# The mLSTM's state update on two halves of the TensorE array: one matmul per head and one copy out of PSUM per direction

## The chip, the cores and the metric

The kernel runs on one core of one Trainium2 chip. The metric is the device time of one execution in microseconds. Before the change three runs took 3370.57, 3371.3 and 3374.14 us, a median of 3371.3 us.

## The reference: what is computed

One encoder layer of width 1024 over 2304 tokens (2048 of one request, 256 of another) with two token mixers side by side, an mLSTM with 8 heads and an attention with 8 query heads and 2 key/value heads, then an output projection, a gated convolutional feed-forward of width 2816 and a last normalisation. The change touches the mLSTM alone. Its core, for one direction (the mLSTM runs forwards and backwards over the sequence), per chunk of tokens and per head:

```python
num = iw[..., None] * jnp.einsum('bhld,bhde->bhle', qb, C) + jnp.einsum('bhls,bhse->bhle', s, vb)
den = iw * jnp.einsum('bhld,bhd->bhl', qb, n) + jnp.sum(s, axis=-1)
h = num / jnp.maximum(jnp.abs(den), jnp.exp(-m_t))[..., None]
C_new = dec[..., None, None] * C + jnp.einsum('bhs,bhsd,bhse->bhde', we, kb, vb)
n_new = dec[..., None] * n + jnp.einsum('bhs,bhsd->bhd', we, kb)
```

The state C is 64 by 64 for each head, and n is a vector of 64. The kernel holds both as one matrix of 64 by 65: a column of ones beside v makes the 65th column of the update the update of n. What the change is about is the second term of C_new and n_new, the product of weighted keys and values.

## The kernel before, in words

The kernel works on chunks of 128 tokens, 18 of them (16 of the first request, 2 of the second), and on pairs of heads, 4 of them. A pair's keys fill 128 partitions or columns: head 0 has 0 to 63, head 1 has 64 to 127. Tensors are kept in float32; where a matmul of full precision is wanted in the fast type, operands are split into a high and a low part (lines 763, 773, 789 and others); the small mLSTM matmuls of lines 842, 887, 893 and 905 take plain float32, which the hardware carries out in two passes each. So each of them stands in the trace as two weight loads and two matmuls.

The stages follow each other: the attention's and gates' projections (to about 250 us), then mLSTM and attention together (to about 1440 us), then the rest of the attention with the output projection (L1045), and from about 1800 us the feed-forward (L1202, L1531). In the second stage two generators are stepped in turn by `run_both`, which compares shares of estimated cost. Of a pair p the mLSTM generator makes: the projections of keys, queries, values and output gate (L763, L773; L789 for the last pair), `projT`, which transposes the keys (L823) and weights them on GpSimd (tile kw, L829), `upd`, which makes each chunk's update (tile mu) and copies it to C (L844, L845), `recur`, which runs the recurrence over the chunks on VectorE (L853), and then the outputs, chunk by chunk: `out_a` (exponentials, L879), `out_b` (tiles mS, L887, and mI, L893), `out_c` (tile mN, L905, and the division), `out_d` (transpose mT, L930, and the store to mix_d). While pair p's outputs are made, pair p+1 is projected. The tiles mu, mS, mI, mN, mT and mt share two PSUM buffers (`MB` = 2, tag "m").

The attention's pieces are in tiles px (a maximum, L573 and L574), ps (scores, L599 and L600), ph and pl (exponentials in two parts, L603 to L605) and pv (values, L617). L617 alternates between a stationary operand of 128 columns and one of 64.

The order of each engine's instructions is made by a scheduler that simulates the program: the mLSTM's small steps are issued under high priority (`MPRI`), and everything else fills in. A change of one instruction's size can therefore move others. In the stage with the output projection the order on TensorE is fixed by hand.

`upd` is called for every chunk and both directions d: forwards the update goes to the next chunk's state, backwards to the previous one's, and where there is none the edge state is cleared. That makes 32 updates per pair and 128 in all. Before the change one matmul multiplies both heads' keys (128 columns) with both heads' values (130 columns), giving a matrix of 128 by 130, of which only the two diagonal blocks of 64 by 65 are wanted. Two copies on ScalarE take them out.

Of the kernel before, what the change touches and what calls it, by code (L numbers as in the profile page):

```python
# [11 lines left out]
AF = mybir.ActivationFunctionType  # L12
# [706 lines left out]
def mlstm(g, tc, s1, sp, sw, sn, pj_, pm):  # L719


    nc = g.nc
# [8 lines left out]
    def weights(p):  # L731
        s = Pair()
        s.p = p
        s.hs = slice(2 * p, 2 * p + 2)
        s.w = [sw.tile([P, 2, 512], F32R, tag="w", name=f"wm{p}_{c}", bufs=WB) for c in range(NCC)] if p else g.wm0
        for c in range(NCC if p else 0):
            load_split(g, s.w[c][:, 0, :], s.w[c][:, 1, :], g.w_m[p, c], g.raw if c % RWM < 2 else sp,
                       f"rm{p}_{c}", RST, g.n1w[:, c:c + 1], bufs=2 if c % RWM < 2 else RWM - 2)
        s.kT, s.qb, s.va, s.C, s.kw = [], [], [], [], {}
        for i in range(NT):  # L740
            s.C.append(sp.tile([P, 2, 65], F32, tag="C", name=f"C{p}_{i}", bufs=NT))
        for b in range(NB):
            s.kT.append(s1.tile([P, BT], F32, tag="kT", name=f"mkT{p}_{b}", bufs=NB))
            s.qb.append(s1.tile([P, 2, 2, P], F32, tag="qb", name=f"qb{p}_{b}", bufs=NB))
            s.va.append(s1.tile([P, 2, 2, 65], F32, tag="va", name=f"va{p}_{b}", bufs=NB))
        return s
# [86 lines left out]
    def upd(s, i):  # L833
        nm = f"{s.p}_{i}"
        kw = s.kw.pop(i)
        pu = pm.tile([P, 2, 130], F32, tag="m", name="mu" + nm)
        lo, hi = SEGS[0] if i < NT1 else SEGS[1]
        for d, nx in ((0, i + 1), (1, i - 1)):
            if not lo <= nx < hi:
                nc.vector.memset(s.C[lo if d == 0 else hi - 1][:, d, :], 0.0)  # L840
                continue
            nc.tensor.matmul(pu[:, d, :], kw[:, d].rearrange("p h d -> p (h d)"),
                             s.va[i // 2][:, i % 2].rearrange("p h e -> p (h e)"), start=True, stop=True)
            nc.scalar.activation(s.C[nx][0:64, d, :], pu[0:64, d, 0:65], AF.Copy)  # L844
            nc.scalar.activation(s.C[nx][64:128, d, :], pu[64:128, d, 65:130], AF.Copy)  # L845

    def recur(s):
        for (c0, c1) in SEGS:
# [89 lines left out]
    def proj_steps(s):  # L938
        for b in range(NB + 2):
            if b < NB:  # L940
                (proj if s.p < LASTP else proj_kv)(s, b)
                if s.p == LASTP:
                    vback(s, b)
            if 2 <= b:
                with tc.high_priority(offset=MPRI):
                    upd(s, 2 * b - 4)
                    upd(s, 2 * b - 3)
            yield (6 if s.p < LASTP else 3) if b < NB else 0.5
            if 1 <= b <= NB:
                with tc.high_priority(offset=MPRI):  # L950
                    projT(s, b - 1)
            yield (6 if s.p < LASTP else 3) if b < NB else 0.5
# [25 lines left out]
    s = weights(0)  # L978
    yield from proj_steps(s)
    for p in range(4):  # L980
# [3 lines left out]
        if p < 3:  # L984
# [9 lines left out]
            s = s2  # L994
# [782 lines left out]
```

## Time and profile before

| What | Value |
|---|---|
| median of three runs | 3371.3 us |
| profiled execution, its own time | 3373.21 us |
| its span, first to last instruction | 3371.5 us |
| mean granted TensorE clock | 0.987 |
| TensorE matmul busy | 3274.1 us (97%) |
| ScalarE busy | 1779.4 us (53%) |
| VectorE busy | 2421.2 us (72%) |
| copies of the updates (L844, L845) | 256, 56.1 us busy |
| update matmuls (L842) in the trace | 256, two per update |

In the rows of the profile PE is TensorE's matmul, PEld its weight load, DVE VectorE, ACT ScalarE, POOL GpSimd and SP SyncE. A tile such as `mu<-va,kw` is output, then inputs; `128*128 128x130` behind a matmul is rows by columns of the stationary operand, and then partitions by moving columns. A matmul's duration runs from its issue to its modelled end; successive ones overlap, so that the distance between their starts, not the duration, is what each costs the engine.

### The profile page before, as it was taken

The numbers are of one execution on the slowest core, as the hardware profiler recorded it, in microseconds if no ns is written. First come the engines' busy times: TensorE is split into PE (matmuls) and PEld (weight loads), VectorE is DVE, ScalarE is ACT, GpSimd is POOL, SyncE is SP. The second block draws the span as 40 slices with busy tenths as digits, with TensorE's granted clock in tenths as the row PEclk, the third lists the DMA queues.
The fourth block names the chain that finished last, engine by engine and source line by source line (L and its number), as shares of the span: only waits on it lengthen the run. The fifth ranks groups of instructions, "written<-read, shape, count | busy, mean of one in ns | idle before, by whom it ended". The sixth has DMA issues, their size and how long they took to land. (4 is left out here: it accounts for less than half of the span.)

```text
span 3371.5 us, 57154 instructions
## 1 busy us (share of the span) xinstructions
PE 3274.1 (97%) x21402; PEld 3047.9 (90%) x21402; DVE 2421.2 (72%) x3771; ACT 1779.4 (53%) x3708; POOL 1311.9 (39%) x1672
## 2 busy tenths in 40 slices
PE   7989999999999999899999999999999999999998
PEld 6878888888888888788889999999999998999998
DVE  6975687777768778876765778878877776544573
ACT  4535666667666776665553544445555555323331
POOL 6544122213232332211245457745555442851112
PEclk9999999999999999999999999999999999999999
DMA  6766343333345444433347334325322223875573
GB/s 223 240 198 175 90 130 102 103 105 116 105 117 176 130 132 138 129 99 97 108 138 260 123 102 148 129 94 180 105 94 94 100 97 103 296 275 172 169 226 100
DMA packets 300262, 481.86 MB, mean 143 GB/s; under 512 B 36528, under 2 KB 186192, under 8 KB 299984
## 3 DMA queue, kind: packets, MB, share of 16 engines
q1 hardware_dynamic: 247600, 348.33, 32.6%
q0 software_dynamic: 35824, 120.42, 10.8%
q10 hardware_dynamic: 16560, 9.44, 0.9%
q8 instruction: 169, 2.77, 0.3%
q14 instruction: 109, 0.89, 0.1%
HBM read 336.19 MB, written 141.90 MB: 142 GB/s over the span
## 5 line engine op out<-in xcount | busy, mean ns | idle before, releaser
L605 DVE TENSOR_TENSOR pl<-ps,ph 128x512 fp32r<-128x512 f32 x520 | 353.3, 684 | 184.1 <-ACT ps L604 176.5
L1202 PE MATMUL pa<-nt,wut 128*128 128x290 f32 (+1 forms) x3168 | 448.3, 297 | 9.2 <-ACT u L1220 7.6
L1202 PEld LDWEIGHTS pa<-nt,wut 128*128 128x128 f32 x3168 | 432.4, 190 | 11.5 <-ACT u L1220 9.4
L603 ACT ACTIVATE ph<-ps 128x512 fp32r<-128x512 f32 x520 | 309.7, 596 | 246.5 <-PE ps L600 240.9
L574 DVE TENSOR_REDUCE mx<-px 128x1 f32<-128x512 f32 (+1 forms) x528 | 346.3, 673 | 73.9 <-PE px L573 71.9
L1312 DVE SCALAR_TENSOR_TENSOR y<-u,cw,y 128x1152 f32<-128x1152 f32 (+1 forms) x176 | 321.4, 1826 | 36.3 <-ACT yc L1310 17.3
L617 PE MATMUL pv<-ph,v 128*128 128x512 f32 (+1 forms) x1040 | 318.6, 400 | 1.5 <-ACT ph L603 1.3
L604 ACT ACTIVATE ps<-ps 128x512 f32<-128x512 f32 x520 | 310.1, 596 | 0.0
L1531 PE MATMUL et<-tet,wet 128*128 128x384 f32 x1584 | 279.2, 337 | 1.1 <-DVE tet L1374 1.1
L1531 PEld LDWEIGHTS et<-tet,wet 128*128 128x128 f32 x1584 | 276.9, 188 | 1.4 <-DVE tet L1374 1.4
L1045 PEld LDWEIGHTS po<-cmx,wo 128*128 128x128 f32 x1728 | 221.8, 192 | 10.0 <-DVE cmx L1033 1.5
L1045 PE MATMUL po<-cmx,wo 128*128 128x256 f32 x1728 | 226.3, 285 | 1.8 <-DVE cmx L1033 1.3
L1531 PE MATMUL e<-te,we 128*128 128x384 f32 x1188 | 212.9, 340 | 9.9 <-ACT te L1373 7.1
L1531 PEld LDWEIGHTS e<-te,we 128*128 128x128 f32 x1188 | 210.4, 190 | 11.0 <-ACT te L1373 7.3
L599 PE MATMUL ps<-qq,kk 128*128 128x512 f32 x520 | 215.4, 416 | 3.7 <-DVE mx L574 2.3
L573 PE MATMUL px<-kk,qq 128*128 128x512 f32 (+1 forms) x528 | 202.1, 412 | 5.2 <-DVE mx L574 2.9
L600 PE MATMUL ps<-qm,kl 65*128 65x512 f32 x520 | 206.8, 400 | 0.0
L763 PE MATMUL mj<-mn,wm 128*128 128x256 f32 x1296 | 202.0, 287 | 2.6 <-ACT og L777 1.9
L763 PEld LDWEIGHTS mj<-mn,wm 128*128 128x128 f32 x1296 | 185.7, 191 | 20.0 <-ACT og L777 2.0
L773 PEld LDWEIGHTS mv<-wm,mn 128*128 128x128 f32 x1296 | 184.2, 191 | 18.5 <-ACT qb L769 2.5
L773 PE MATMUL mv<-wm,mn 128*128 128x256 f32 x1296 | 197.9, 286 | 1.0 <-ACT qb L769 0.9
L617 PEld LDWEIGHTS pv<-ph,v 128*128 128x128 f32 (+1 forms) x1040 | 157.0, 163 | 38.3 <-ACT ph L603 2.6
(305 smaller groups left out, 7245.2 us busy)
## 6 DMA issues: line engine op xcount, KB each, us to landing
mn<-n_d SPq DMA_DIRECT2D x216, 256.0 KB, 3.3
ru<-w_up SPq DMA_DIRECT2D x88, 512.0 KB, 3.6
a_d<-y POOLq DMA_DIRECT2D x88, 288.0 KB, 2.6
a_d<-tc POOLq DMA_DIRECT2D x66, 288.0 KB, 3.0
n_d<-n1T SPq DMA_DIRECT2D x18, 1024.0 KB, 5.6
dm<-nm_d POOLq DMA_DIRECT2D x72, 256.0 KB, 4.0
mjn<-n_d SPq DMA_DIRECT2D x72, 256.0 KB, 3.3
mvn<-n_d SPq DMA_DIRECT2D x72, 256.0 KB, 3.2
```

Source lines behind the costliest of these rows:

```text
L574: nc.vector.tensor_reduce(s.mx[:, t, z0:z0 + 1], ps[:, 0:w], AX.X, ALU.max)
L599: nc.tensor.matmul(ps, kk[:, kc:kc + P], s.qq[:, 0:N], start=True, stop=False)
L603: nc.scalar.activation(ph, ps, AF.Exp)
L604: nc.scalar.activation(ps, ps, AF.Exp)
L605: nc.vector.tensor_tensor(pl, ps, f32(ph), ALU.subtract)
L617: nc.tensor.matmul(s.pv[0:HD if k in (1, 3) else P, 0:N], v, p, start=(kp == 0 and k == 0), stop=(2 * kp + 2 == s.nk and k == 5))
L763: nc.tensor.matmul(pj[:, o], s.w[c][:, a, o * P:(o + 1) * P], nT[c][:, :, h, :], start=(c + o + k == 0), stop=(c == NCC - 1 and k == 2 and ...
L773: nc.tensor.matmul(pv[:, o], nT[c][:, o, a, :], s.w[c][:, h, 256:512], start=(c + o + k == 0), stop=(c == NCC - 1 and k == 2 and o == 1))
L1045: nc.tensor.matmul(po[:, o], wo[z // 2][c][:, a, n], mx[c][:, h, :], start=(c == 0 and k == 0), stop=(c == NCC - 1 and k == 2))
L1202: nc.tensor.matmul(p[:, z], w[:, aa, c, :], ops[k][:, c, bb, z * m:z * m + m], start=c == 0 and i == 0 and not add, stop=c == NCC // 2 - 1 ...
L1312: nc.vector.scalar_tensor_tensor(y[:, s:e], u[:, s + k:e + k], cw[:, k, jj:jj + 1], y[:, s:e], ALU.mult, ALU.add)
L1531: nc.tensor.matmul(ps[m // 2][:, m % 2], w[:, aa, m * P:(m + 1) * P], t[:, bb], start=p == 0 and n == 0, stop=p == NP - 1 and n == 2)
```

## The change

Each update's matmul of 128 by 130 is replaced by two, one per head: head h's 64 key columns as stationary operand, placed at columns 64h of the array, and head h's 65 value columns as moving operand. The result of head h lands in partitions 64h to 64h+63 and in columns 0 to 64, for both heads. So a single copy of 128 by 65 takes both out of PSUM. The PSUM tile keeps its size. Nothing else is edited.

```diff
@@ upd(s, i), inside the loop over (d, nx) @@
-            nc.tensor.matmul(pu[:, d, :], kw[:, d].rearrange("p h d -> p (h d)"),
-                             s.va[i // 2][:, i % 2].rearrange("p h e -> p (h e)"), start=True, stop=True)
-            nc.scalar.activation(s.C[nx][0:64, d, :], pu[0:64, d, 0:65], AF.Copy)
-            nc.scalar.activation(s.C[nx][64:128, d, :], pu[64:128, d, 65:130], AF.Copy)
+            for h in range(2):
+                r = slice(64 * h, 64 * h + 64)
+                nc.tensor.matmul(pu[r, d, 0:65], kw[:, d, h], s.va[i // 2][:, i % 2, h], start=True, stop=True,
+                                 tile_position=(0, 64 * h))
+            nc.scalar.activation(s.C[nx][:, d, :], pu[:, d, 0:65], AF.Copy)
```

The diff adds one line, so that lines behind it carry numbers one higher afterwards (L905 becomes L906). TensorE issues 20,780 matmuls where it issued 20,652, ScalarE 128 instructions fewer; on the other engines the number is the same.

On TensorE, at the first updates of the first pair (a minus stands for before, a plus for the change):

```order
-L842 MATMUL mu_0_3325<-va_0_2525,kw_0_3138 128x130
-L842 MATMUL mu_1_3330<-va_0_2525,kw_1_3140 128x130
+L844 MATMUL mu_0_3325<-va_0_2525,kw_0_3138 64x65 x2
+L844 MATMUL mu_1_3330<-va_0_2525,kw_1_3140 64x65 x2
 L763 MATMUL mj_4_3785<-mn_4_0_3769,wm_0_395 128x256 x6
 L763 MATMUL mj_4_3785<-mn_4_1_3770,wm_1_508 128x256 x6
-L763 MATMUL mj_4_3785<-mn_4_2_3771,wm_2_629 128x256 x5
+L763 MATMUL mj_4_3785<-mn_4_2_3771,wm_2_629 128x256 x6
```

Each row of an update becomes two matmuls in the same place. Here two updates stand in a row; counted over the program, the 128 updates stand in 96 such groups with other matmuls between them, 32 of them of two updates. Behind 89 of these groups stands a matmul with an ordinary load of 128 columns, behind the other 7 a transpose.

On ScalarE, at the copies of those updates:

```order
-L844 ACTIVATE C_1_2506<-mu_0_3325 64x65
-L845 ACTIVATE C_1_2506<-mu_0_3325 64x65
-L844 ACTIVATE C_2_2507<-mu_1_3330 64x65
-L845 ACTIVATE C_2_2507<-mu_1_3330 64x65
+L846 ACTIVATE C_1_2506<-mu_0_3325 128x65
+L846 ACTIVATE C_2_2507<-mu_1_3330 128x65
 L603 ACTIVATE ph_0_0_0_2909<-ps_0_0_0_2906 128x512
 L604 ACTIVATE ps_0_0_0_2906<-ps_0_0_0_2906 128x512
```

Four copies of 64 partitions become two of 128, ahead of the attention's exponentials.

On TensorE again, at the last chunk's outputs of the last pair. Before:

```order
L617 MATMUL pv_8_18666<-pl_8_1_1_17561,v_16_0_11404 128x512
L905 MATMUL mN_17_18460<-va_8_13697,dm_17_18331 128x65 x4
L930 MATMUL mT_15_18480<-ident,hh_15_18399 128x128
L599 MATMUL ps_8_4_0_18703<-qq_8_17195,kk_16_8_11424 128x512
L600 MATMUL ps_8_4_0_18703<-qm_8_17197,kl_16_8_11425 128x512
```

And with the change:

```order
L617 MATMUL pv_8_18666<-pl_8_0_1_17470,v_16_0_11404 128x512
L906 MATMUL mN_17_18460<-va_8_13697,dm_17_18331 128x65 x4
L599 MATMUL ps_8_3_0_18674<-qq_8_17195,kk_16_4_11413 128x512
L600 MATMUL ps_8_3_0_18674<-qm_8_17197,kl_16_4_11414 128x512
L599 MATMUL ps_8_3_1_18682<-qq_8_17195,kk_16_4_11413 128x512
L600 MATMUL ps_8_3_1_18682<-qm_8_17197,kl_16_4_11414 128x512
```

The attention's pieces stand earlier or later against the mLSTM's: the last mN now follows the values (pl) of one pair of key blocks earlier, and attention work stands between it and mT_15. Such shifts, of up to 68 matmuls, run through the whole stage; the output projection and the feed-forward keep the order that they had but for a few rows.

## The prediction

> **What bounds the kernel now.** I read the page's head first, then the stretches of the stage in which the update stands, then the groups of the lines that the diff touches, then the waits.
>
> ```profile
> span 3371.5 us, 57154 instructions
> PE 3274.1 (97%) x21402; PEld 3047.9 (90%) x21402; DVE 2421.2 (72%) x3771; ACT 1779.4 (53%) x3708; POOL 1311.9 (39%) x1672
> core 0: us, PE busy (x) PEld busy (x) DVE busy (x) ACT busy (x) POOL busy (x), PEclk, DMA share, GB/s
> 290.00:1275.00 985.00, 979.68 (x6211) 857.89 (x6210) 739.62 (x1593) 664.53 (x1790) 260.89 (x532) 1.00 0.40 119
> 1275.00:1440.00 165.00, 154.96 (x927) 131.47 (x927) 142.77 (x355) 111.09 (x298) 47.16 (x90) 0.96 0.43 127
> ```
>
> In the stretch that holds all updates (290 to 1275 us) TensorE is busy 979.68 of 985 us at full clock. ScalarE is busy 664.53 us, two thirds of it. So the stage is as long as TensorE's list of work: a nanosecond more or less on TensorE counts nearly whole, one on ScalarE only where TensorE waits for it. TensorE's idle time there is 5.3 us, all that a faster ScalarE could win at the level of gaps.
>
> ```profile
> L842 PEld LDWEIGHTS mu<-va,kw x256: 186/189/193, 295.2 to 1273.4; 128*128 128x128 f32 x128
> L842 PE MATMUL mu<-va,kw x256: 272/274/378, 295.4 to 1273.5; 128*128 128x130 f32 x128
> L844 ACT ACTIVATE C<-mu 64x65 f32<-64x65 f32 x128 | 27.7, 217 | 46.1 <-PE mu L842 43.4 <-DMA mn<-n_d 1.3
> L845 ACT ACTIVATE C<-mu 64x65 f32<-64x65 f32 x128 | 28.4, 222 | 1.5
> ```
>
> The 128 updates are 256 passes on TensorE, and 256 copies on ScalarE that take 56.1 us. The first copy of each pair waits for TensorE, not the other way round.
>
> **The copies.** A copy of 65 columns takes 217 to 222 ns. The shape that replaces it, 128 partitions by 65, is in no row; a copy's time I take from its columns, so 128 copies of some 220 ns go and 28 us of ScalarE go with them. Their cover is named above: TensorE runs 99% of the stretch regardless. What comes out is read from the waits of TensorE and its loads on ScalarE between 290 and 1440 us, of which these name the copies or the largest of the rest:
>
> ```profile
> PE pv L617 <- ACT ph L603: 1.3, 2, 1.0
> PE mN L905 <- ACT C L845: 0.3, 1, 0.3
> PEld pv L617 <- ACT ph L603: 2.6, 5, 1.2
> PEld mN L905 <- ACT C L845: 1.2, 3, 0.7
> PEld mT L930 <- ACT C L845: 0.6, 2, 0.4
> PEld mu L842 <- ACT C L845: 0.3, 1, 0.3
> ```
>
> The waits on C come from the two PSUM buffers that mu shares with mS, mI, mN and mT: 2.4 us. An update's two directions hold their buffer for four copies today, for two afterwards, which halves them: −1.2 us. The exponentials wait behind fewer copies, worth perhaps −0.3 us of the 3.9. I take −1.5 us. Bounds: 0, and −6.3 us if all six rows vanished.
>
> **The matmuls.** What a pass costs is the distance between starts. Three pieces of the timeline show it: an update, the outputs' mN with 65 moving columns, and the transposes of L428.
>
> ```profile
> 309.25 0.42 PEld L842 LDWEIGHTS mu<-va,kw 128*128 128x128 f32 x2
> 309.60 0.19 PEld L599 LDWEIGHTS ps<-qq,kk 128*128 128x128 f32 x1
> 309.71 0.19 PEld L600 LDWEIGHTS ps<-qm,kl 65*128 65x128 f32 x1
> 309.49 0.38 PE L842 MATMUL mu<-va,kw 128*128 128x130 f32 x2
> 449.73 0.53 PEld L905 LDWEIGHTS mN<-va,dm 128*128 128x128 f32 x4
> 450.17 0.19 PEld L599 LDWEIGHTS ps<-qq,kk 128*128 128x128 f32 x1
> 450.28 0.19 PEld L600 LDWEIGHTS ps<-qm,kl 65*128 65x128 f32 x1
> 246.27 0.39 PEld L428 LDWEIGHTS gpt<-ident,rows 40*128 40x128 f32 x5
> ```
>
> Update: two matmuls in 0.38 us, one lasting 0.27, so 110 ns between them, and the next load starts 110 ns on (309.60 to 309.71). One update costs 2 x 110 = 220 ns. mN: four loads in 0.53 us of 0.19 each, 113 ns apart, and L599's load and its successor again 110 ns apart (450.17 to 450.28), though only 65 columns move. So a load of 128 float32 columns sets 110 ns, whatever moves above it.
>
> ```profile
> L617 PEld LDWEIGHTS pv<-ph,v 128*64 128x64 f32 x520 | 70.5, 136 | 15.1
> L617 PEld LDWEIGHTS pv<-pl,v 128*128 128x128 f32 x520 | 98.0, 189 | 27.7
> L905 PE MATMUL mN<-va,dm x576: 217/275/447, 449.4 to 1433.9; 128*128 128x65 f32 x192
> ```
>
> A load of 64 columns is 189 − 136 = 53 ns shorter than one of 128: it sets about 55 ns. The fastest 65-column matmul (217) is 55 ns shorter than the 130-column one (272): half the columns also stream in 55 ns. So a new pass needs 55 ns for its load and 55 ns for its stream, side by side. Whether the engine issues a load and a matmul that often, L428 answers: five loads in 0.39 us of 0.14, 62 ns apart. The pass costs 55 to 62 ns, an update four of them: 220 to 248 ns against 220. That is 0 to +28 ns, 128 times: 0 to +3.6 us, of which I take +1.8 by the middle.
>
> The last pass adds a cost of its own. Today the next matmul's load (110 ns) hides under the update's last stream of 110 ns; behind a stream of 55 ns it sticks out by 55, as behind mN. It happens once per group of updates with an ordinary load behind it, by the order 89 times: 89 x 55 ns = +4.9 us. Bounds: 0, if a free half of the array lets that load begin earlier, and the 4.9. The entrance costs nothing either way: its load hides under a predecessor of 110 ns or more. Matmuls: +6.7 us, from 0 to +8.5.
>
> **Narrow stationary operands as such.** Two rows could speak of a cost of changing the array's division. L617 alternates 128 and 64 columns 520 times. And L323, 40 columns wide, whose program gives it the same tile of 128 by 64 as the new matmuls:
>
> ```profile
> 99.40 0.14 PEld L323 LDWEIGHTS pg<-ident,gp 128*40 128x40 f32 x2
> 99.55 0.30 PEld L249 LDWEIGHTS pj<-w_a,n1T 128*128 128x128 f32 x2
> 99.44 0.38 PE L323 MATMUL pg<-ident,gp 128*40 128x128 f32 x2
> 99.57 0.48 PE L249 MATMUL pj<-w_a,n1T 128*128 128x512 f32 x1
> ```
>
> L249's load starts 110 ns after L323's second matmul (99.44 plus 0.11, the 0.38 less one duration of 0.27), and the next load 110 ns later (0.30 less 0.19). Nothing waits for an empty array, so I put the change of division at nothing. Column position 64 is in no row; that is what keeps the rival below alive.
> The Trainium skill, TensorEngine Tiling (Array Packing), section Tiling Modes, speaks against the change: changing the tiling mode drains the engine. By this rule the sum would be the drain rival's; the rows of L617 and L323 do not show it.
>
> **Order.** The scheduler moves work by up to 68 matmuls. In a stretch where TensorE is full, order is free. It is not at the end of the mLSTM, where the last outputs' chain makes TensorE wait:
>
> ```profile
> 1400.00:1420.00 20.00, 14.25 (x60) 10.58 (x61) 19.05 (x52) 12.28 (x36) 5.25 (x11) 0.74 0.26 80
> 1406.86 1.94 PE L905 MATMUL mN<-va,dm 128*128 128x65 f32 x8 [3.11 <-DVE mmx L935]
> ```
>
> VectorE is busy 19.05 of 20 us there and TensorE 14.25, at a clock of 0.74; one mN stands 3.11 us behind mmx on VectorE. With the change less attention work stands between the last mNs, and some between mN and mT_15. I can't sign this: the gaps of such a stretch, 5.75 us here, are the size of it, so ±3 us, taken as 0.
>
> **Sum.** −1.5 + 1.8 + 4.9 + 0 = +5.2 us. On the profiled execution, whose own time is 3373.21 us (its span of 3371.5 and 1.7 around it), that gives 3378.4. This execution was 1.9 us above the median of 3371.3, so for a median I say 3376.5 us, +0.15%. What this kernel's measurement can tell from no change is about 0.2%, 6.7 us.
>
> **The rivals.** *The array drains at each change of division.* An update's matmul lasts 272 ns where its successor starts after 110; the difference of about 160 ns is what an emptied array would cost, at the entrance and the exit of 96 groups: 192 x 0.16 = +31 us, with the 5.2 some 3407 us. Against it stand the rows of L617 and L323. Loads that don't overlap the streams of the other half give a like sum: four passes of 110 ns instead of 55, +220 ns x 128 = +28 us. It decides from about 35 ns per change on (6.7 us over 192). Chance 0.13.
>
> *The two heads run beside each other in the two halves.* Head 1's passes overlap head 0's and an update costs two passes of 55 ns instead of four: −110 ns x 128 = −14 us on the sum, 3362 us. For it: they share no columns. Against it: loads follow each other in one row of the trace everywhere, and four loads at 55 ns are already the 220. Chance 0.10.
> The Trainium skill says so in TensorE: Matmul & The Clock Gate, section Part 3: Packing small matmuls: matmuls in different column groups run concurrently, some 4 ns apart. No run here shows it.
>
> *ScalarE's relief or the new order wins more than TensorE loses.* The waits on ScalarE vanish whole (−6.3 instead of −1.5 us), and the chain at the end loses the 3.11 us wait and its like. −6.3 + 6.7 − 6 gives −6 us, 3365.5 us. For it speaks that ScalarE loses 28 us of 664; against it that only 2.4 us of the waits name the copies. Chance 0.15.
>
> **How the numbers follow.** The forecast has 0.62, spread over 0 to +10 us by its own bounds; about a third of that lies above the 6.7 us. Slower: 0.13 + 0.22 = 0.35. Faster: 0.07 of the concurrent case and 0.06 of the last one = 0.13. Same: the remaining 0.52. The range must hold 0.8: from 3363 us, which leaves out half of the concurrent case, to 3392, which takes in a drain of half the price and leaves the full one out. The forecast's own range is 3369 to 3382.
>
> **What would show it.** The new matmuls' rows should stand 55 to 62 ns apart, four to an update, and the load behind them 110 ns from its successor, with the matmul behind a group starting late by some 55 ns. The copies: 128 of about 220 ns. TensorE's busy share up to 1275 us should stay at 99%. Distances of 110 ns or more between the passes, or a hole at a group's edges, mean the drain; starts a few ns apart mean that the heads run together; a shorter stretch with unchanged TensorE work means the relief or the order. If the stretch after 1275 us carries the difference, my mechanism is wrong whatever the total.

## The result and the profile after

The change makes the kernel slower: 3393.38 us (median of four runs, 3387.08 to 3393.99) against 3372.72 us for the kernel before (four runs). The ratio is 1.0063, with a 95% interval of 1.0051 to 1.0075: +21 us, between +17 and +25. The prediction had 3376.5 us as the likeliest time and 3392 us as the upper end of its range.

The page's head and the stretches of the mLSTM's stage, of the kernel after:

```profile
span 3390.8 us, 57505 instructions
PE 3287.6 (97%) x21658; PEld 3036.2 (90%) x21658; DVE 2419.2 (71%) x3771; ACT 1749.9 (52%) x3580; POOL 1318.0 (39%) x1672
290.00:1275.00 985.00, 980.37 (x6373) 837.92 (x6372) 725.28 (x1561) 626.16 (x1645) 259.54 (x528) 1.00 0.39 117
1275.00:1440.00 165.00, 158.08 (x957) 135.21 (x956) 138.62 (x348) 108.21 (x286) 44.14 (x85) 0.94 0.46 137
```

ScalarE lost 29.5 us, as it should. TensorE's busy share in the long stretch is what it was, 980.37 us of 985 after 979.68: a matmul counts as busy until its modelled end, so a TensorE on which nothing streams for a tenth of a microsecond still looks busy. The loads show the cost. The groups of the updates' loads, of the kernel before and then after (busy, mean ns, and behind the second bar the load engine's idle time ahead of them):

```profile
L842 PEld LDWEIGHTS mu<-va,kw 128*128 128x128 f32 x256 | 40.4, 190 | 7.3 <-issue 2.3 <-ACT C L845 0.3
```

```profile
L844 PEld LDWEIGHTS mu<-va,kw 128*64 128x64 f32 x512 | 22.8, 135 | 29.1 <-issue 21.1 <-ACT ps L604 1.4 <-ACT ph L603 1.0
L846 ACT ACTIVATE C<-mu 128x65 f32<-128x65 f32 x128 | 25.4, 226 | 41.6 <-PE mu L844 40.3 <-DMA mn<-n_d 0.9
```

Idle time ahead of the updates' loads rises from 7.3 to 29.1 us, and 21.1 of it is "issue": time in which the load waited for nothing that the profile names. The copies are as forecast, 128 of 226 ns.

The two kernels have the same update between the same neighbours, a 64-column matmul of L617 ahead and L599 behind. Before (the fence of the prediction has its loads), the matmuls:

```profile
309.25 0.39 PE L617 MATMUL pv<-ph,v 128*64 128x512 f32 x1
309.49 0.27 PE L842 MATMUL mu<-va,kw 128*128 128x130 f32 x1
```

After, a group of one update (start, time, engine and line), loads first:

```profile
308.99 0.20 PEld L844 LDWEIGHTS mu<-va,kw 128*64 128x64 f32 x4 [0.42 <-issue]
309.26 0.19 PEld L599 LDWEIGHTS ps<-qq,kk 128*128 128x128 f32 x1
309.37 0.19 PEld L600 LDWEIGHTS ps<-qm,kl 65*128 65x128 f32 x1
308.67 0.40 PE L617 MATMUL pv<-ph,v 128*64 128x512 f32 x1
308.99 0.34 PE L844 MATMUL mu<-va,kw 128*64 128x65 f32 x4
308.99 0.28 PE L844 MATMUL mu<-va,kw 128*64 128x65 f32 x2
```

Before, L617 starts at 309.25, the update at 309.49, and L599 has its weights at 309.71, when the next load may start: 0.46 us for L617's stream of 0.23 and an update of 0.22. After, the same way goes from 308.67 to 309.37, 0.70 us. Step by step:

- The first loads of the update start 0.32 us behind L617, not under its stream. The stream ends after 0.23, so nothing streams for 0.09 us, and then the load takes some 0.05 with nothing streaming above it (the distance of 0.11 to the next pair of matmuls is a load and a stream of 0.055 each).
- Two matmuls start at once (the window around 308.99 holds two rows in 0.28 us, one lasting 0.27, so they start within 10 ns of each other) and two more 0.11 us on: head 0 and head 1 run side by side, and an update streams in 0.11 us instead of 0.22.
- The last pair starts at 309.11 (308.99 + 0.34 less one duration of 0.22) and streams 0.05. L599's load starts only at 309.26, 0.10 us behind that, and takes 0.11 us, again with nothing above it.

A group of two updates pays the edges once (loads, then matmuls, of the kernel after):

```profile
325.57 0.31 PEld L844 LDWEIGHTS mu<-va,kw 128*64 128x64 f32 x8 [0.37 <-issue]
325.95 0.19 PEld L599 LDWEIGHTS ps<-qq,kk 128*128 128x128 f32 x1
326.06 0.19 PEld L600 LDWEIGHTS ps<-qm,kl 65*128 65x128 f32 x1
325.24 0.40 PE L600 MATMUL ps<-qm,kl 65*128 65x512 f32 x1
325.57 0.45 PE L844 MATMUL mu<-va,kw 128*64 128x65 f32 x8
```

325.24 to 326.06 is 0.82 us where 0.23 + 2 x 0.22 = 0.67 were needed before. So the edges of a group cost 0.09 + 0.05 + 0.10 + 0.11 = 0.35 us, and each update in it saves 0.11. Taken in the same way over every group of both traces (from the start of the matmul ahead to the start of the stream behind, less the stream ahead), the median is 462 ns for a group of one, where it was 225, and 580 ns for a group of two, where it was 448. With the 64 and 32 groups that the order has: 64 x 0.237 + 32 x 0.132 = 19.4 us. That is the measured 21 within its interval, though the order has a share in where the time appears (see the point on the order).

### The profile page after: what moved, and what is told of

The parts are those of the page before. It is cut to its first block, busy times and chain, and to the rows that moved or that the text cites. A ratio compares the mean times of both kernels' runs of the same rounds, so it can differ in the third digit from the quotient of the medians.

```text
span 3390.8 us, 57505 instructions
## 1 busy us (share of the span) xinstructions
PE 3287.6 (97%) x21658; PEld 3036.2 (90%) x21658; DVE 2419.2 (71%) x3771; ACT 1749.9 (52%) x3580; POOL 1318.0 (39%) x1672
## 5 line engine op out<-in xcount | busy, mean ns | idle before, releaser
L617 PE MATMUL pv<-ph,v 128*128 128x512 f32 (+1 forms) x1040 | 318.4, 400 | 0.5 <-ACT ph L603 0.5
L599 PE MATMUL ps<-qq,kk 128*128 128x512 f32 x520 | 216.2, 418 | 2.2 <-DVE pl L605 1.4
L573 PE MATMUL px<-kk,qq 128*128 128x512 f32 (+1 forms) x528 | 203.8, 416 | 3.3 <-DVE mx L574 2.0
L773 PEld LDWEIGHTS mv<-wm,mn 128*128 128x128 f32 x1296 | 183.6, 190 | 19.6 <-ACT qb L769 2.3
L773 PE MATMUL mv<-wm,mn 128*128 128x256 f32 x1296 | 198.4, 285 | 1.2 <-ACT qb L769 1.2
L617 PE MATMUL pv<-pl,v 128*128 128x512 f32 x520 | 189.7, 397 | 0.0
```

Source lines behind the costliest of these rows:

```text
L599: nc.tensor.matmul(ps, kk[:, kc:kc + P], s.qq[:, 0:N], start=True, stop=False)
L617: nc.tensor.matmul(s.pv[0:HD if k in (1, 3) else P, 0:N], v, p, start=(kp == 0 and k == 0), stop=(2 * kp + 2 == s.nk and k == 5))
L773: nc.tensor.matmul(pv[:, o], nT[c][:, o, a, :], s.w[c][:, h, 256:512], start=(c + o + k == 0), stop=(c == NCC - 1 and k == 2 and o == 1))
```

## The experiments

Theory after the result: any plain float32 matmul with 64 stationary columns divides the array, nothing streams for a while when the division changes, and all of the loss stands at the groups' edges. Rivals: the copies or ScalarE's queue; the number of small matmuls; columns 64 to 127; the scheduler's new order. Each run is compared with runs of the kernel before on the same chip; 0.1% is 3.4 us.

### The copy alone

```diff
 nc.tensor.matmul(pu[:, d, :], ...)            # as before: 128 by 130
-nc.scalar.activation(s.C[nx][0:64, d, :], pu[0:64, d, 0:65], AF.Copy)
-nc.scalar.activation(s.C[nx][64:128, d, :], pu[64:128, d, 65:130], AF.Copy)
+nc.scalar.activation(s.C[nx][:, d, :], pu[:, d, 0:65], AF.Copy)
```

> The update's matmul of before (128 by 130, whole array), with the change's single copy of 128 by 65. Left out: head 1's block is not taken out, so head 1's state is wrong. The drain theory (the 20 us come from the gaps ahead of and behind each group of 64-column matmuls) expects no gaps and the time of before, 0 to -2 us for the 128 copies that go. The rival, that a lighter ScalarE or the new order sets the time, expects a clear move here: -6 us if relief counts, or a good part of the +20 us if the scheduler's new order is what costs.

Measured: 0.9998 (0.9988 to 1.0008), no change. Its copies:

```profile
L844 ACT ACTIVATE C<-mu 128x65 f32<-128x65 f32 x128 | 26.0, 225 | 42.5 <-PE mu L842 40.6 <-DMA mn<-n_d 1.1
```

128 copies fewer, 30 us of ScalarE, are worth between −4 and +3 us of the kernel, and the order that this run has shows no cost either. Beyond that bound the copies are out, as a gain and as a loss.

### The matmuls alone

```diff
 (the change's two matmuls)
-nc.scalar.activation(s.C[nx][:, d, :], pu[:, d, 0:65], AF.Copy)
+for h in range(2):
+    r = slice(64 * h, 64 * h + 64)
+    nc.scalar.activation(s.C[nx][r, d, :], pu[r, d, 0:65], AF.Copy)
```

> The change's two matmuls per update at array columns 0 and 64, but a copy per head as before (two of 64 by 65). The drain theory expects the change's time, +20 to +23 us over before, with the same gaps (load 326 ns behind the start of a 512-column matmul, +248 ns for a group of one update, +149 ns for a group of two; 64 and 32 such groups stand in the order, 20.6 us). The rival, that the wider copy or its place in ScalarE's queue costs the time, expects about 0.

Measured: 1.0082 (1.0066 to 1.0097), +22 to +33 us. The whole loss comes with the matmuls. Its median for a group of one is 464 ns and for two 582, those of the change. The first matmul of the output projection starts at the same time as with the change; the rows of the change and then of this run:

```profile
L1046 PE MATMUL po<-cmx,wo x1728: 274/282/416, 1460.0 to 1852.5; 128*128 128x256 f32 x192
```

```profile
L1048 PE MATMUL po<-cmx,wo x1728: 274/282/419, 1460.2 to 1860.2; 128*128 128x256 f32 x192
```

In the profiled executions what this run takes longer than the change comes behind 1460 us, where no update stands; why is not shown.

### Both heads at columns 0 to 63

```diff
-nc.tensor.matmul(pu[r, d, 0:65], kw[:, d, h], ..., tile_position=(0, 64 * h))
+nc.tensor.matmul(pu[0:64, d, 65 * h:65 * h + 65], kw[:, d, h], ...)
...
+for h in range(2):
+    nc.scalar.activation(s.C[nx][64 * h:64 * h + 64, d, :], pu[0:64, d, 65 * h:65 * h + 65], AF.Copy)
```

> Both heads' matmuls at array columns 0 to 63, results side by side in PSUM partitions 0 to 63, a copy per head that moves head 1's to partitions 64 to 127. Theory A, that any plain float32 matmul on 64 columns changes the array's division and drains it: the same gaps stay (about 95 ns and a load of 54 at the entrance, about 100 and a load of 108 at the exit), and the two heads can no longer run side by side, which adds 110 ns per update: 46 groups of one update at 358 ns and 41 of two at 369 ns, +32 us. Theory B, that array columns 64 to 127 are what drains: no gaps, four passes of 55 to 62 ns per update and 55 ns of load behind each group, +5 to +8 us.

Measured: 1.0096 (1.0082 to 1.0109), +32 us, theory A's number. A group of one between a transpose and a projection (loads, then the transpose's matmuls):

```profile
302.14 0.31 PEld L843 LDWEIGHTS mu<-va,kw 128*64 128x64 f32 x4 [0.17 <-ACT ph L603]
302.51 0.30 PEld L763 LDWEIGHTS mj<-mn,wm 128*128 128x128 f32 x2
301.83 0.38 PE L823 MATMUL mt<-ident,mkT 128*128 128x128 f32 x2
```

The transposes' second matmul starts at 301.94 (301.83 + 0.38 less one duration of 0.27) and streams 0.11, to 302.05; the update's first load comes at 302.14, 0.09 later: the same gap, without columns 64 to 127 and without a named position. (The row names a wait on ACT here, but over all 87 groups the median of the gap is 0.09 to 0.10 us, as in the change.) The four loads stand 58 ns apart (0.31 less one of 0.14, over three). That is the 55 to 62 ns of the prediction for a pass, and nothing runs side by side. The medians of the groups are 576 and 807 ns, 351 and 360 above before, with 46 and 41 groups 31 us.

### The whole array for both

```diff
+for h in range(2):
+    nc.tensor.matmul(pu[:, d, 65 * h:65 * h + 65], kw[:, d].rearrange("p h d -> p (h d)"), s.va[i // 2][:, i % 2, h], ...)
 (two copies as before)
```

> Two matmuls per update as in the change, 65 moving columns each, but both with the whole stationary operand of 128 columns (no division of the array), and the two copies of before. The drain theory expects no gap at the groups' edges, and passes 110 ns apart, paced by loads of 128 columns: four per update instead of two, 128 x 220 ns = +28 us, all of it inside the groups. A theory by which twice as many small matmuls bring the gaps, whatever their width, expects the change's gaps on top: +45 us and more.

Measured: 1.0084 (1.0070 to 1.0097), +24 to +33 us around the expected 28. Loads, then matmuls:

```profile
308.91 0.65 PEld L843 LDWEIGHTS mu<-va,kw 128*128 128x128 f32 x4
309.48 0.19 PEld L573 LDWEIGHTS px<-kk,qq 128*128 128x128 f32 x1
308.68 0.63 PE L617 MATMUL pv<-ph,v 128*128 128x512 f32 x2
309.15 0.55 PE L843 MATMUL mu<-va,kw 128*128 128x65 f32 x4
```

As many matmuls as in the change, and no gap: the first load goes under L617's stream (308.91 lies 0.23 behind its first start), and the last load of the four starts 0.11 us ahead of L573's (308.91 + 0.65 less one of 0.19 is 309.37, against 309.48). A whole-array pass costs the 110 ns of its load of 128 columns although only 65 move. This run costs as much as the divided version, in another place, and here the reckoned time of TensorE shows in the total.

### The updates in larger groups

```diff
-upd(s, 2 * b - 4)
-upd(s, 2 * b - 3)
+upd2(s, 2 * b - 4)    # both chunks: eight matmuls, each queued behind the first; then the four copies
```

> The change with the updates of two chunks issued together, up to four updates (eight matmuls) in a row, one PSUM tile for both chunks; the order has 36 groups instead of 96, 24 of four updates, 8 of three and 4 of two. The drain theory: a group pays its gaps once and each update in it costs 110 ns instead of 220, so against before about -80 ns for a group of four, +30 for three, +140 for two: -1 us in sum, so the 20 us vanish though every matmul and copy of the change is there. A theory by which each new matmul costs more by itself, or the order does, expects +15 to +20 us still.

Measured: 1.0034 (1.0022 to 1.0047), +11 us. Neither −1 nor +20. A group of four updates, loads:

```profile
308.50 0.55 PEld L847 LDWEIGHTS mu<-va,kw 128*64 128x64 f32 x16 [0.25 <-issue]
309.12 0.20 PEld L823 LDWEIGHTS mt<-ident,mkT 128*128 128x128 f32 x2
```

Sixteen loads in 0.55 us: the updates themselves do what was expected, with medians of 764 ns for four updates (before about 2 x 448 = 896), 648 for three and 826 for the 4 groups of two, which hold waits of another kind as well (a group of two took 580 in the change). Over 36 groups that is 24 x 0.764 + 8 x 0.648 + 4 x 0.826 = 26.8 us, where before took 70 x 0.225 + 29 x 0.448 = 28.7. So the change's loss is gone, and another stands elsewhere. The last mN and the output projection of the kernel before, and of this run:

```profile
L905 PE MATMUL mN<-va,dm x576: 217/275/447, 449.4 to 1433.9; 128*128 128x65 f32 x192
L1045 PE MATMUL po<-cmx,wo x1728: 274/282/561, 1442.7 to 1839.1; 128*128 128x256 f32 x192
```

```profile
L912 PE MATMUL mN<-va,dm x576: 217/275/477, 445.1 to 1409.3; 128*128 128x65 f32 x192
L1051 PE MATMUL po<-cmx,wo x1728: 274/282/561, 1452.7 to 1845.5; 128*128 128x256 f32 x192
1410.00:1452.00 42.00, 32.60 (x89) 20.08 (x89) 35.77 (x72) 23.08 (x53) 5.24 (x7) 0.67 0.47 141
```

The mLSTM ends 25 us earlier and the output projection starts 10 us later. In the 42 us between, the attention runs alone: TensorE is busy 32.60 us at a clock of 0.67, VectorE 35.77. The scheduler put the last outputs' steps ahead and left 20 us of TensorE's own work behind them, where before had 7.

### The lead of the mLSTM over the attention

The lead is the constant by which `run_both` chooses which generator to step next (`LEAD = 1.3`). Three runs, of the grouped version and of the kernel before:

> The grouped version with the mLSTM's lead over the attention set to 1.35 instead of 1.3 (run_both), so that as much work stands behind the last update in TensorE's order as before the change (150 us by TensorE's own pace, against 168 in the first grouped version) and the last outputs have attention work between them and little behind them. If the 11 us of the first grouped version come from attention standing alone behind the mLSTM's end, they go: -2 to +3 us against before. If they belong to the groups, +11 us stay.

> The grouped version with a lead of 1.32, between the two: 14 us of TensorE's work behind the last mN, against 20 in the first grouped version and 4 with 1.35. If the order of the mLSTM's end is what costs, this one lies between: 0 to +8 us against before.

> The kernel before with the lead of 1.35 alone: what the lead does without the change. By the theory that the end of the mLSTM is a matter of order, it moves a few us either way, -4 to +4; the updates cost 220 ns each as before.

Measured: grouped with 1.35: 1.0026 (1.0015 to 1.0038), +9 us. Grouped with 1.32: 1.0021 (1.0010 to 1.0032), +7 us. Before with 1.35: 1.0056 (1.0044 to 1.0069), +19 us. The first and the last miss what was expected of them; the second lies in its range, but not between the two others. Against the +11 of the first grouped version 2 to 4 us less is within the intervals nothing. And the lead alone, without any change to an update, costs as much as the change under study. At 1.35 the kernel before starts its output projection early (1425.4 us) and ends it late:

```profile
L1045 PE MATMUL po<-cmx,wo x1728: 274/282/562, 1425.4 to 1851.8; 128*128 128x256 f32 x192
```

So more of the attention is left for that stage, and the loss shows by its end. What the order does to the total is a matter of 10 to 20 us in this kernel, and none of these orders brings the grouped version to before. The section on float32r on the whole array comes back to where this time may go.

### Float32r at columns 0 to 63

```diff
-kw = s1.tile([P, 2, 2, 64], F32, ...)          # va likewise, padded to 66 columns
+kw = s1.tile([P, 2, 2, 64], F32R, ...)
...
+nc.tensor.matmul(pu[0:64, d, 66 * h:66 * h + 66], kw[:, d, h], s.va[i // 2][:, i % 2, h], ...)
 (a copy per head)
```

> Two matmuls per update of 64 stationary columns at array columns 0 to 63, as in the run with both heads there, but of type float32r: weighted keys and values are rounded to it, and a padded 66th column keeps the count even; a copy per head. Changed in the computation: the keys' and values' precision in the state and in the outputs. By type: the 64-column matmul of L617 is float32r and showed no gap, so here too no gap at the groups' edges, one pass per matmul instead of two, 55 to 62 ns each: 110 to 124 ns per update instead of 220, plus 55 to 80 ns of load behind each of 99 groups: -14 us + 7 us, -5 to -9 us. If the width of 64 columns changes the array's division whatever the type, the gaps stay, some 250 ns more per group: +15 to +20 us.

Measured: 0.9990 (0.9978 to 1.0001): −7 to 0 us, with the gain not clear of zero. The gaps are gone. Loads, then the matmuls ahead:

```profile
308.38 0.25 PEld L843 LDWEIGHTS mu<-va,kw 128*64 128x64 f32 x2
308.55 0.30 PEld L773 LDWEIGHTS mv<-wm,mn 128*128 128x128 f32 x2
308.02 0.63 PE L773 MATMUL mv<-wm,mn 128*128 128x256 f32 x4
308.50 0.25 PE L843 MATMUL mu<-va,kw 128*64 128x66 f32 x2
```

The first of the 64-column loads starts at 308.38 while L773's last matmul has just started (308.02 + 0.63 less one duration of 0.28 is 308.37), and L773's next load 0.02 us behind the second update matmul's start (308.50 + 0.25 less a duration of 0.22 is 308.53), not 0.10 behind the end of its stream. The medians are 170 and 288 ns per group, 55 and 160 below before. The same 64 columns at the same place, of the other type (and so with one pass instead of two), show no gap.

### Float32r on the whole array

```diff
-kw, va: F32; one matmul of 128 by 130, two passes
+kw, va: F32R; one matmul of 128 by 130, one pass
```

> The kernel before with one matmul of 128 by 130 on the whole array per update, and two copies, but weighted keys and values rounded to float32r: one pass of 110 ns per update instead of two, no gap at any edge. Changed in the computation: the precision of keys and values, as in the other float32r run. The updates themselves lose 128 x 110 ns = 14 us. If TensorE's time counts whole, -10 to -14 us. The order puts 21 us of TensorE's work behind the last mN, as in the first grouped version, where attention alone behind the mLSTM's end went with +11 us; if that order costs the same here, -2 to -5 us remain.

> The float32r version on the whole array with a lead of 1.34, which leaves 9 us of TensorE's work behind the last mN in the order instead of 21, close to the 7 of before. If attention alone at the mLSTM's end ate the rest of the 14 us, they come out here: -10 to -14 us against before. If the lead costs by itself, as it did in the kernel before (+19 us at 1.35), 0 to +10 us.

Measured: 0.9984 (0.9975 to 0.9993), −5.4 us; with the lead of 1.34, 0.9981 (0.9972 to 0.9990), −6.4 us. Both are faster than the kernel before and than the change, at the price of the rounding of keys and values to float32r. The updates give 14 us by the passes that are gone, of which 8 to 9 do not arrive. The first of the two fits the reckoning with an order like that of the first grouped version; the second, whose order leaves 9 us behind the last mN, was to bring the rest and brought 1 us, within both intervals nothing. So the work behind the last mN doesn't by itself explain the rest.

The granted clock goes with what is missing. These rows show the end of the mLSTM in six runs: before, the change, the first grouped version, before with the lead of 1.35, float32r on the whole array, and the same with 1.34. The third number from the end is the clock.

```profile
1380.00:1480.00 100.00, 88.28 (x498) 71.84 (x497) 87.89 (x200) 63.13 (x157) 21.18 (x37) 0.93 0.43 130
1380.00:1480.00 100.00, 87.81 (x477) 71.27 (x476) 87.38 (x208) 62.92 (x159) 22.48 (x41) 0.88 0.49 145
1380.00:1480.00 100.00, 80.85 (x357) 59.67 (x356) 81.94 (x166) 50.48 (x113) 15.43 (x21) 0.80 0.30 91
1380.00:1480.00 100.00, 81.31 (x442) 68.88 (x442) 74.90 (x167) 48.27 (x121) 20.14 (x33) 0.81 0.38 117
1380.00:1480.00 100.00, 86.39 (x385) 64.61 (x385) 79.11 (x149) 49.81 (x106) 14.16 (x20) 0.81 0.25 75
1380.00:1480.00 100.00, 90.27 (x478) 72.00 (x479) 79.31 (x153) 52.62 (x117) 18.82 (x24) 0.91 0.30 91
```

The clock is 0.80 or 0.81 in three versions that stay behind what their updates give. It is 0.91 in the profiled execution of the lead of 1.34, and that execution took 3357.96 us, 15 us less than the profiled one of before (3373.21): there the 14 us arrive. Over all executions the mean clock was 0.9887 before and 0.9842, 0.9852, 0.9857 and 0.9873 in the last four versions. An estimate from these figures: if TensorE could have used every share of the clock that it lost, the four lose 15, 12, 10 and 5 us by it, against the 13, 19, 9 and 8 us that they stay behind. So the lower clock can account for much of the rest. No run changes the clock alone, and the grouped version with the lead of 1.35, with 0.90 in that window, is still 9 us slower than before; as a cause it is not shown.

## Why the prediction was wrong, point by point

**That TensorE's time counts whole** fits the whole-array run, reckoned at +28 us and measured at +24 to +33, and the change, whose groups give 19.4 us of the measured 21. It isn't shown in general: of the 14 us that the float32r runs save, 5 to 6 arrived.

**The copies** are not contradicted: taken at −1.5 us, measured between −4 and +3, with 128 copies of 225 to 226 ns.

**The passes.** 55 to 62 ns per pass was right where passes follow each other (58 ns with both heads at columns 0 to 63). In the change they don't: the heads' matmuls start within 10 ns of each other, and an update streams in 0.11 us instead of the 0.22 to 0.25 of the term. The term should have been −14 us instead of +1.8. This is the rival of the two heads beside each other, which had 0.10. The prediction held against it that loads follow each other; but the loads of the two halves go in pairs as well, four in 0.20 us and eight in 0.31.
The Trainium skill, TensorE: Matmul & The Clock Gate, section Part 3: Packing small matmuls, has matmuls of different column groups start some 4 ns apart; the rows here allow up to 10 ns, so the trace agrees.

**The load behind the group** was right as a mechanism and its 0.055 us was too small: the load stands there with its whole 0.11 us, because it starts only 0.10 us behind the end of the stream.

**The change of division put at nothing** is the step that failed. It rested on L617 and L323, which have 64-column tiles and show no gap. (The reading of L323 has a slip that doesn't change it: L249's load starts with L323's second matmul, at 99.55, and not 110 ns behind it.) The float32r run shows why L617 was no precedent: with that type the updates' 64 columns show no gap either. And in the group after the change the gap stands between L617's own 64 columns and the update's. L323 is a transpose. Neither is a plain float32 matmul of the update's kind, and no matmul of plain float32 with 64 columns or fewer, other than transposes, stood in the kernel before. That it is the transpose that spares L323 the gap no run here tests. The rows of the profile print f32 for all three, so that the type has to be read from the kernel's lines, which the prediction did not do. The gaps are 0.09 us at the entrance and 0.10 at the exit, where the drain's rival had reckoned 0.16 each; with the loads that stand free (0.05 and 0.11) an edge pair costs 0.35 us, and 96 of them 34 us. Less the 14 us of the heads side by side, that is +20 of the measured +21.
The Trainium skill, TensorEngine Tiling (Array Packing), section Tiling Modes, says that changing the mode drains the engine: the trace agrees, against the way in which the prediction weighed it. The same page's section Restrictions and Gotchas names the transpose mode of float32 and float32r as incompatible with column tiling, which fits L323.

**The rivals** were taken as excluding each other. The drain (+31) and the two heads beside each other (−14) are two sides of the same division of the array, and came together. Their sum with the prediction's own terms, 5.2 + 31 − 14, would have been +22. That it comes so close is in part luck: the gaps were reckoned too long and the loads behind them too short.

**The order** was put at ±3 us. The change's own order can't be told apart from the edges by the total, since its groups' sum fills the result, but the trace says that it has a share:

```profile
L844 PE MATMUL mu<-va,kw x512: 220/222/272, 294.8 to 1284.0; 128*64 128x65 f32 x171
```

The last update stands at 1273.5 us before and at 1284.0 with the change, the first matmul of the output projection at 1442.7 and 1460.0. So 10.5 of the 17.3 us are there by the last update, and the rest comes in the stretch behind it, where no update stands, the order differs and the clock is 0.88 instead of 0.93. By these rows a part of the edges' 19.4 us didn't arrive in their own stretch, and about as much came in behind it; how the two are linked is not shown. The prediction's own sign, that a difference behind 1275 us would speak against its mechanism, was met in part. As a bound for this kernel ±3 us was far too narrow: the grouped version and the lead show 7 to 19 us.

## What to carry to other kernels

Dividing TensorE's array costs per visit: here 0.35 us of edges against 0.11 us saved per update, so by this reckoning it gains only from four updates in a row on (0.35 / 0.11 = 3.2). Count the visits in the order before counting the matmuls, and look for a precedent of the same type, not only of the same width. TensorE's busy share did not show these gaps (979.68 and 980.37 us of 985); the idle time ahead of the loads did (7.3 and 29.1 us). And compare the granted clock of two runs before putting a difference down to their work.

## What the runs showed of the hardware that was not expected

- A plain float32 matmul with 64 stationary columns had these gaps even at columns 0 to 63 and without a named position; a float32r matmul of that width had none. With the gaps, the first 64-column load starts 0.09 us behind the end of the stream ahead of it, and the first load of 128 columns 0.10 us behind the end of the last small stream.
- With the heads at columns 0 and 64, their float32 passes interleave: eight matmuls of 65 columns take 0.45 us up to the end of the last one, 0.22 us of which is that one's own duration.
- A single constant that sets the order of two generators moved the kernel before by 19 us, nearly as much as the change itself. Its mean granted clock went from 0.9887 to 0.9852 with it.
